# Decay masks by biased exponentials on ScalarE instead of subtractions and products on VectorE

## The chip, the cores and the metric

The kernel runs on one core of a Trainium2 chip. The metric is the device time of one execution in microseconds (us). The engines are named as in the profile: PE (TensorE matmul) and PEld (its weight loads), DVE (VectorE), ACT (ScalarE), POOL (GpSimd) and SP (SyncE, which issues the DMAs). Each engine runs its instructions in the order in which the program gives them, and an instruction that waits holds up all behind it on its engine.

## The reference

The model is two layers of a backbone for 256 context and 512 latent tokens of width 1024. In each layer one input projection feeds four head groups in parallel: A, windowed attention with a sink logit per head; B, dense attention; C, a bidirectional mLSTM in chunks; D, a bidirectional Mamba-2 in chunks of 128 tokens. Their outputs go through one output projection, and a squared-ReLU MLP follows.

Three things matter here. In A the softmax of a head is taken with one more logit, the sink: with m = max(scores/8, sink), the row is exp(score/8 - m), and its sum has exp(sink - m) added. In D, for each head h and direction d, the contribution of token s to token t of a chunk is weighted by

```
mask[s, t] = exp(cum[t] - cum[s]) * dt[s]      for t >= s (forward) or t <= s (backward), else 0
```

where cum is a running sum of decays and dt = softplus(...) is the step size. In C the weight is exp(-(b[s, t] - a[s])) with the same triangles. Since dt > 0, the D mask can also be written as exp(cum[t] + (ln dt[s] - cum[s])).

## The kernel before

Tokens are held in six chunks of 128 (two of context, four of latents). Layer 0 makes output for all six, layer 1 (`need` is False) for the four latent chunks. The head groups run one after the other, A first, then D, C and B; dense projections of a later group are cut into pieces and put between the steps of the group that runs (`fill(...)`), so that PE has work while DVE and ACT prepare the next step. Then come output projection and MLP, which are almost all matmuls. The program is written in the order of the dependences; a scheduler with priorities sets the final order of each engine's instructions, and pools of tiles (CB, MB and pr share one of four buffers) set when a buffer is free again.

The names that the change and the prediction touch:

- `attend_s` (from L619): scores and softmax of a pair of heads. `m` is the row maximum, `es` the sink's term, `pr` the probabilities, `den` (dn in the trace) their sum, `R` its reciprocal. `attend_v` transposes the probabilities into `pth`, `ptl` and multiplies by V; then `tm` and `yA` are A's output.
- `gates()` (L798 to L888): a generator whose steps are run between others. It makes `u` (48 columns of gate logits and 48 of dt), `cum`, `aS`, `D3`, later `E` and `crP`; rows of cumulative sums go to a DRAM buffer, `drv`.
- `fD` and `thd`: D's projections after convolution and gate. `btok`, `xtok`: their transposes. `hst`: the state of D. `adr`: a piece of the modulation.
- The D loop (L1026 to L1070), per chunk j: `CB` (128 x 2 directions x 4 heads x 128) is loaded by DMA as broadcast rows of cum, POOL fills the wrong triangle with -1e30 (L1033, L1034), DVE subtracts cum per partition, ACT takes the exponential, DVE (layer 0) or POOL (layer 1) multiplies by dt and adds the directions to `W`; DVE multiplies W by the raw product, and PE multiplies W by `xtok`. `yi` and `ysk` lead to `zs`; after the loop `zs` is scaled by `ssD` (L1073), transposed and evacuated to `yD`.
- The C loop (L1255 on), per chunk: `MB` is loaded and filled likewise, DVE subtracts `aS`, ACT takes the exponential, DVE multiplies by the raw product. `yC` is C's output; `qB`, `kB` and `bsq` belong to the projections of B that run beside it.

The helpers L95 (`mm`), L103 (`act`), L106 (`tt`), L110 and L111 (`ts`) and L114 (`stt`) record most instructions, so lines of the trace are often those.

Of the kernel before, what the change touches and what calls it, by code (L numbers as in the profile page):

```python
# [9 lines left out]
I32 = mybir.dt.int32  # L10
# [12 lines left out]
DEPTH = 2  # L23
EPS = 1e-6
BIG = 1e30

C_BADA, C_G1, C_G2, C_CW, C_CB, C_GM, C_GS, C_GB, C_GF = 0, 48, 56, 64, 82, 88, 90, 92, 94
NPC = 102
# [15 lines left out]
def tile_hybrid_backbone(ctx, tc, xin, cin, wada, wopen, win0, win, wout, wf1, wf2, pcol, prow, cst, rope, out):  # L44
# [444 lines left out]
    for l in range(DEPTH):  # L489
# [123 lines left out]
            return rp  # L613

        eos, khl = {}, {}
        gb = pc_[:, C_GB:C_GB + 2]
        rq = sm((P, NJ, 4), "rq")

        def attend_s(a, kv, j):  # L619
# [17 lines left out]
            for e in range(2):  # L637
                sp = s2()
                q = eo[:, e, js]
                for b in range(nb):  # L640
                    segs = []
                    lo_, hi_ = b * half, (b + 1) * half
                    if lo_ < NX:
                        segs.append((0, lo_, min(hi_, NX) - lo_))
                    if hi_ > NX:
                        s0 = max(lo_, NX)
                        segs.append((s0 - lo_, b0 + s0 - NX, hi_ - s0))
                    if len(segs) == 2 and segs[1][1] == segs[0][1] + segs[0][2]:
                        segs = [(0, segs[0][1], segs[0][2] + segs[1][2])]
                    mms = []  # L650
                    for part in range(2):
                        for o_, s_, n_ in segs:
                            mms.append((sp[:, b, o_:o_ + n_], q, KH[:, part, s_:s_ + n_]))
                    if a == "A":
                        for i, bl in enumerate(blocks):
                            if bl >= 2 and bl != j:
                                mk = mkp if bl < j else mkn
                                k0, k1 = i * P, (i + 1) * P
                                s0, s1 = max(k0, lo_), min(k1, hi_)
                                if s0 < s1:  # L660
                                    mms.append((sp[:, b, s0 - lo_:s1 - lo_], idb, mk[:, s0 - k0:s1 - k0]))
                    for i, (o_, l_, r_) in enumerate(mms):
                        mm(o_, l_, r_, i == 0, i == len(mms) - 1)
                sv = sp[:, 0:nb, 0:half]
                me, de = m1[:, e:e + 1], den[:, e:e + 1]
                hd = 2 * kv + e
                V.tensor_reduce(me, sv, AX.XY, ALU.max)
                if a == "A":
                    sk = pr_[:, R_SINK + hd:R_SINK + hd + 1]
                    ts(me, me, 0.125, sk, ALU.mult, ALU.max)  # L670
                    tt(es[:, e:e + 1], sk, me, ALU.subtract)
                    ts(me, me, -1.0, None, ALU.mult)
                    scale = 0.125
                else:
                    scale = rq[:, j, hd:hd + 1]
                    stt(me, me, -1.0, scale, ALU.mult, ALU.mult)
                pr = k4((P, nk), name="pr")
                act(pr.rearrange("p (b n) -> p b n", b=nb), sv, AF.Exp, bias=me, scale=scale, accum=de)
                Ps.append(pr)
            if a == "A":  # L680
                act(es, es, AF.Exp)
                tt(den, den, es, ALU.add)
            V.reciprocal(den, den)
            R = th_((P, P), name="R")
# [113 lines left out]
        def gates():  # L798
# [18 lines left out]
            act(an, pr_[:, R_ALOG:R_ALOG + 8], AF.Exp)  # L817
            ts(X[:, :, 0:8], u[:, :, 0:8], -1.0, None, ALU.mult)
            stt(X[:, :, 8:16], u[:, :, 8:16], -1.0, an.unsqueeze(1).to_broadcast([P, NJ, 8]), ALU.mult, ALU.mult)
            yield  # L820
            cp = bulk((P, 192))
            mm(cp[:, 0:48], cs[:, K_LE:K_LE + P], X[:, :, 0::2])
# [62 lines left out]
            V.tensor_copy(D3[:, 2], tot[:, :, 8:16])  # L885
            act(D3, D3, AF.Exp)
            tt(D3[:, 1], D3[:, 1], dt[:, :, 8:16], ALU.mult)
            yield  # L888

        gsteps = gates()  # L890
# [136 lines left out]
        for ji, j in enumerate(out_tok):  # L1027
# [4 lines left out]
                         drv[2:4, j * 512:(j + 1) * 512].unsqueeze(0).to_broadcast([P, 2, 512]))  # L1032
            G.affine_select(out=CB[:, 0], in_=CB[:, 0], pattern=[[0, 4], [1, P]], compare_op=ALU.is_ge, fill=-BIG, base=0, channel_multiplier=-1)  # L1033
            G.affine_select(out=CB[:, 1], in_=CB[:, 1], pattern=[[0, 4], [-1, P]], compare_op=ALU.is_ge, fill=-BIG, base=0, channel_multiplier=1)  # L1034
            tt(CB, CB, bc(cum[:, j, 8:16].rearrange("p (h d) -> p d h", d=2), (P, 2, 4, P)), ALU.subtract)
            act(CB, CB, AF.Exp)
            W_ = ta((P, 4, P), name="W")
            GV = V if need else G
            GV.tensor_tensor(CB, CB, bc(dt[:, j, 8:16].rearrange("p (h d) -> p d h", d=2), (P, 2, 4, P)), ALU.mult)
            GV.tensor_tensor(W_, CB[:, 0], CB[:, 1], ALU.add)  # L1040
            Wg = W_.rearrange("p (g h) t -> p g h t", g=2)
            tt(Wg, Wg, raw.unsqueeze(2).to_broadcast([P, 2, 2, P]), ALU.mult)
            fill(wa * fD_)
# [23 lines left out]
        yD = k6(4, (P, 2, NT), name="yD")  # L1067
        for j in out_tok:
            js = slice(j * P, (j + 1) * P)
            ts(zs[:, j, :], zs[:, j, :], ssD[:, j:j + 1], None, ALU.mult)  # L1070
            yp = mx((P, 256))
            for m in range(2):
                TE.transpose(yp[:, m * P:(m + 1) * P], zs[:, j, m * P:(m + 1) * P], ident)  # L1073
# [181 lines left out]
        for ji, j in enumerate(out_tok):  # L1255
# [4 lines left out]
            SY.dma_start(MBf, drv[0:2, j * 512:(j + 1) * 512].unsqueeze(0).to_broadcast([P, 2, 512]))  # L1260
            G.affine_select(out=MB[:, 0], in_=MB[:, 0], pattern=[[0, 4], [1, P]], compare_op=ALU.is_ge, fill=BIG, base=0, channel_multiplier=-1)
            G.affine_select(out=MB[:, 1], in_=MB[:, 1], pattern=[[0, 4], [-1, P]], compare_op=ALU.is_ge, fill=BIG, base=0, channel_multiplier=1)
            tt(MB, MB, bc(aS[:, j].rearrange("p (h d) -> p d h", d=2), (P, 2, 4, P)), ALU.subtract)
            act(MB, MB, AF.Exp, scale=-1.0)
            MBe = MB.rearrange("p d (e q) t -> p d e (q t)", e=2)
            tt(MBe, MBe, raw[:, :, 0:256].unsqueeze(1).to_broadcast([P, 2, 2, 256]), ALU.mult)
            fill(wa * fC_ if ji < nout - 1 else FILL_CB[l][4])
# [330 lines left out]
```

## Time and profile before

| | before |
|---|---|
| runs, median (lowest, highest) | 1860.95 us (1854.97, 1861.11) |
| profiled execution, own time | 1865.19 us |
| its span | 1862.9 us |
| mean granted PE clock | 0.969 |
| PE, DVE, ACT, POOL busy | 1776.5, 1227.1, 866.1, 331.4 us |

Busy time is an average over the whole span. It doesn't tell how the stages differ: in the MLP PE is the only engine that counts, and among the head groups the engines wait for each other. The granted clock is a share of 2.4 GHz. A wait is put down to the instruction that released it last.

### The profile page before, as it was taken

How to read it: one execution, taken by the hardware profiler on the slowest of the kernel's cores; microseconds unless marked ns; L12 is line 12 of the kernel's file. 1: busy time of each engine (PE TensorE's matmuls, PEld its weight loads, DVE VectorE, ACT ScalarE, POOL GpSimd, SP SyncE). 2: the span in 40 equal slices, each digit the busy share in tenths (PEclk: the TensorE clock that was granted, in tenths of full speed). 3: DMA queues.
4: the chain of work that ended last, by engine and by line, in shares of the span. 5: the costliest groups of instructions: out<-in, count | busy, mean ns of one | idle time of the engine just before them, and what ended most of it. 6: DMA issues, size and time to landing. Idle time of an engine off the chain costs nothing.

```text
span 1862.9 us, 31119 instructions
## 1 busy us (share of the span) xinstructions
PE 1776.5 (95%) x11754; PEld 1556.4 (84%) x11754; DVE 1227.1 (66%) x2765; ACT 866.1 (46%) x1820; POOL 331.4 (18%) x322
## 2 busy tenths in 40 slices
PE   7999999989999999999999989989989899999997
PEld 4898888878788888888888888879768799999997
DVE  3588875688877566466466576886588765555555
ACT  4655523356656464344345356542456543333333
POOL 1200111220014363142243311033120200000000
PEclk8999999799999999999999989999989899999999
DMA  8233442321123343342332411132221122332222
GB/s 315 80 103 105 147 129 86 104 97 52 35 80 109 97 130 102 97 130 97 100 121 97 138 62 53 46 93 86 74 69 52 40 91 92 96 96 92 91 93 66
DMA packets 97813, 178.85 MB, mean 96 GB/s; under 512 B 10752, under 2 KB 19328, under 8 KB 97664
## 3 DMA queue, kind: packets, MB, share of 16 engines
q1 hardware_dynamic: 97664, 176.88, 29.8%
q8 instruction: 92, 1.51, 0.3%
q14 instruction: 57, 0.47, 0.1%
HBM read 172.51 MB, written 4.33 MB: 95 GB/s over the span
## 4 chain that ended last, share of the span: by engine, by line
PE 79%; DVE 8%; ACT 5%; DMA 3%; issue 2%; POOL 2%; SPq 0%; DVEq 0%; ACTq 0%; POOLq 0%
PE bulk L95 39%; PE s L95 29%; PE mx L95 8%; PE mx L706 2%; ACT wh L103 1%; DVE wl L106 1%; DMA CB<-drows 1%; DVE x L114 1%; DMA adar<-in_wada_dram 1%; ACT qs L103 1%; POOL acc L296 1%; ACT pr L103 1%; DMA x<-in_xin_dram 1%; ACT pth L103 0%; DVE EO L106 0%
## 5 line engine op out<-in xcount | busy, mean ns | idle before, releaser
L106 DVE TENSOR_TENSOR wl<-wraw,wh 128x512 fp32r<-128x512 f32 (+2 forms) x400 | 286.5, 721 | 117.1 <-ACT wh L103 109.2
L103 ACT ACTIVATE wh<-wraw 128x512 fp32r<-128x512 f32 (+2 forms) x400 | 239.6, 610 | 265.4 <-PE bulk L95 139.4
L95 PE MATMUL s<-h,wh 128*128 128x258 f32 (+2 forms) x1040 | 316.6, 314 | 0.0
L95 PE MATMUL s<-hl,wh 128*128 128x258 f32 (+2 forms) x1040 | 305.9, 313 | 0.0
L95 PE MATMUL s<-h,wl 128*128 128x258 f32 (+2 forms) x1040 | 252.1, 312 | 0.0
L95 PE MATMUL bulk<-ah,wh 128*128 128x512 f32 (+1 forms) x576 | 218.1, 379 | 4.1 <-DVE mod L106 2.8
L95 PE MATMUL bulk<-ah,wl 128*128 128x512 f32 (+1 forms) x576 | 215.9, 375 | 0.0
L95 PE MATMUL bulk<-al,wh 128*128 128x512 f32 (+1 forms) x576 | 215.8, 375 | 0.0
L296 POOL TENSOR_TENSOR acc<-acc,adap 128x512 f32<-128x512 f32 x96 | 142.3, 1489 | 410.6 <-ACT acc L103 238.9
L95 PEld LDWEIGHTS s<-h,wh 128*128 128x128 f32 x1040 | 197.2, 190 | 20.8
L114 DVE SCALAR_TENSOR_TENSOR x<-bulk,mod,x 128x512 f32<-128x512 f32 (+1 forms) x224 | 149.4, 670 | 98.4 <-PE bulk L95 97.3
L95 PEld LDWEIGHTS s<-hl,wh 128*128 128x128 f32 x1040 | 197.7, 190 | 11.8 <-issue 0.2
L95 PEld LDWEIGHTS s<-h,wl 128*128 128x128 f32 x1040 | 165.9, 190 | 1.3
L95 PE MATMUL bulk<-h,wh 128*128 128x512 f32 (+1 forms) x416 | 154.2, 371 | 0.9 <-DVE KHL L106 0.5
L95 PE MATMUL bulk<-hl,wh 128*128 128x512 f32 (+1 forms) x416 | 145.3, 349 | 0.0
L95 PE MATMUL bulk<-h,wl 128*128 128x512 f32 (+1 forms) x416 | 145.2, 349 | 0.0
L95 PEld LDWEIGHTS bulk<-ah,wh 128*128 128x128 f32 x576 | 108.3, 188 | 25.3 <-DVE mod L106 4.6
L95 PEld LDWEIGHTS bulk<-ah,wl 128*128 128x128 f32 x576 | 108.2, 188 | 21.3
L95 PEld LDWEIGHTS bulk<-al,wh 128*128 128x128 f32 x576 | 108.3, 188 | 19.3
L103 ACT ACTIVATE relu<-relu,bs 128x512 f32<-128x512 f32 x96 | 58.8, 644 | 127.6 <-DVE relu L106 127.6
L103 ACT ACTIVATE adap<-adar,silw 128x256 f32<-128x256 f32 x192 | 85.0, 497 | 52.5 <-DMA adar<-in_wada_dram 52.5
L95 PE MATMUL bulk<-wh,h 128*128 128x256 f32 (+1 forms) x336 | 105.4, 314 | 3.0 <-ACT h L103 1.7
(355 smaller groups left out, 3809.1 us busy)
## 6 DMA issues: line engine op xcount, KB each, us to landing
wraw<-in_wf_dram SPq DMA_DIRECT2D x256, 256.0 KB, 2.7
adar<-in_wada_dram SPq DMA_DIRECT2D x96, 256.0 KB, 3.0
wraw<-in_win_dram SPq DMA_DIRECT2D x72, 256.0 KB, 2.9
ada<-in_wada_dram SPq DMA_DIRECT2D x64, 256.0 KB, 4.1
adaw<-in_wada_dram SPq DMA_DIRECT2D x16, 512.0 KB, 6.7
wraw<-in_wout_dram SPq DMA_DIRECT2D x32, 256.0 KB, 3.1
x<-in_xin_dram SPq DMA_DIRECT2D x8, 768.0 KB, 5.4
CB<-drows SPq DMA_DIRECT2D x10, 512.0 KB, 6.0
```

Of the source, the lines that this page charges most:

```text
L95: return TE.matmul(o, lhsT=l, rhs=r, start=start, stop=stop)
L103: return S.activation(o, i, f, scale=scale, **kw)
L106: return V.tensor_tensor(o, a, b, op)
L114: return V.scalar_tensor_tensor(o, a, s, b, op0, op1)
L296: G.tensor_tensor(acc[:, v], acc[:, v], dst, ALU.add)
L706: TE.transpose(tp[:, i, e, :], Ps[e][:, (i0 + i) * P:(i0 + i + 1) * P], ident)
```

## The change

The step size goes into the exponent. `gates()` computes ln(dt) by two Newton steps from a guess out of dt's bits, and keeps u = ln(dt) - cum in the columns of `u` that are free by then. In the D loop the subtraction of cum and the product by dt are gone; one exponential of 1024 columns is replaced by eight of 128, one for each direction and head, with u (a value per partition) as bias. In the C loop the subtraction of aS is gone in the same way. The sum of the two directions, W, is made by DVE in both layers. The scale of zs by ssD goes from DVE to ACT. In A's softmax the negated sinks are prepared once (`nsk`), and three small DVE operations per head become one; the sink's exponential is taken per head, with a bias.

```diff
--- before.py
+++ after.py
@@ -23,6 +23,7 @@
 DEPTH = 2
 EPS = 1e-6
 BIG = 1e30
+LN2 = 0.6931471805599453
 
 C_BADA, C_G1, C_G2, C_CW, C_CB, C_GM, C_GS, C_GB, C_GF = 0, 48, 56, 64, 82, 88, 90, 92, 94
 NPC = 102
@@ -613,6 +614,8 @@
             return rp
 
         eos, khl = {}, {}
+        nsk = sm((P, 4), "nsk")
+        ts(nsk, pr_[:, R_SINK:R_SINK + 4], -1.0, None, ALU.mult)
         gb = pc_[:, C_GB:C_GB + 2]
         rq = sm((P, NJ, 4), "rq")
 
@@ -666,10 +669,8 @@
                 hd = 2 * kv + e
                 V.tensor_reduce(me, sv, AX.XY, ALU.max)
                 if a == "A":
-                    sk = pr_[:, R_SINK + hd:R_SINK + hd + 1]
-                    ts(me, me, 0.125, sk, ALU.mult, ALU.max)
-                    tt(es[:, e:e + 1], sk, me, ALU.subtract)
-                    ts(me, me, -1.0, None, ALU.mult)
+                    ts(me, me, -0.125, nsk[:, hd:hd + 1], ALU.mult, ALU.min)
+                    act(es[:, e:e + 1], nsk[:, hd:hd + 1], AF.Exp, bias=me, scale=-1.0)
                     scale = 0.125
                 else:
                     scale = rq[:, j, hd:hd + 1]
@@ -678,7 +679,6 @@
                 act(pr.rearrange("p (b n) -> p b n", b=nb), sv, AF.Exp, bias=me, scale=scale, accum=de)
                 Ps.append(pr)
             if a == "A":
-                act(es, es, AF.Exp)
                 tt(den, den, es, ALU.add)
             V.reciprocal(den, den)
             R = th_((P, P), name="R")
@@ -817,6 +817,14 @@
             act(an, pr_[:, R_ALOG:R_ALOG + 8], AF.Exp)
             ts(X[:, :, 0:8], u[:, :, 0:8], -1.0, None, ALU.mult)
             stt(X[:, :, 8:16], u[:, :, 8:16], -1.0, an.unsqueeze(1).to_broadcast([P, NJ, 8]), ALU.mult, ALU.mult)
+
+            ln, d_ = u[:, :, 0:8], e[:, :, 0:8]
+            ts(d_, u[:, :, 8:16], 1e-30, None, ALU.max)
+            ts(ln, d_.bitcast(I32), LN2 / 8388608.0, -126.955 * LN2, ALU.mult, ALU.add)
+            for _ in range(2):
+                act(z[:, :, 0:8], ln, AF.Exp, scale=-1.0)
+                tt(z[:, :, 0:8], z[:, :, 0:8], d_, ALU.mult)
+                stt(ln, z[:, :, 0:8], -1.0, ln, ALU.add, ALU.add)
             yield
             cp = bulk((P, 192))
             mm(cp[:, 0:48], cs[:, K_LE:K_LE + P], X[:, :, 0::2])
@@ -885,6 +893,7 @@
             V.tensor_copy(D3[:, 2], tot[:, :, 8:16])
             act(D3, D3, AF.Exp)
             tt(D3[:, 1], D3[:, 1], dt[:, :, 8:16], ALU.mult)
+            tt(u[:, :, 0:8], u[:, :, 0:8], cum[:, :, 8:16], ALU.subtract)
             yield
 
         gsteps = gates()
@@ -1032,12 +1041,11 @@
                          drv[2:4, j * 512:(j + 1) * 512].unsqueeze(0).to_broadcast([P, 2, 512]))
             G.affine_select(out=CB[:, 0], in_=CB[:, 0], pattern=[[0, 4], [1, P]], compare_op=ALU.is_ge, fill=-BIG, base=0, channel_multiplier=-1)
             G.affine_select(out=CB[:, 1], in_=CB[:, 1], pattern=[[0, 4], [-1, P]], compare_op=ALU.is_ge, fill=-BIG, base=0, channel_multiplier=1)
-            tt(CB, CB, bc(cum[:, j, 8:16].rearrange("p (h d) -> p d h", d=2), (P, 2, 4, P)), ALU.subtract)
-            act(CB, CB, AF.Exp)
+            for d in range(2):
+                for h in range(4):
+                    act(CB[:, d, h, :], CB[:, d, h, :], AF.Exp, bias=u[:, j, 2 * h + d:2 * h + d + 1])
             W_ = ta((P, 4, P), name="W")
-            GV = V if need else G
-            GV.tensor_tensor(CB, CB, bc(dt[:, j, 8:16].rearrange("p (h d) -> p d h", d=2), (P, 2, 4, P)), ALU.mult)
-            GV.tensor_tensor(W_, CB[:, 0], CB[:, 1], ALU.add)
+            tt(W_, CB[:, 0], CB[:, 1], ALU.add)
             Wg = W_.rearrange("p (g h) t -> p g h t", g=2)
             tt(Wg, Wg, raw.unsqueeze(2).to_broadcast([P, 2, 2, P]), ALU.mult)
             fill(wa * fD_)
@@ -1067,7 +1075,7 @@
         yD = k6(4, (P, 2, NT), name="yD")
         for j in out_tok:
             js = slice(j * P, (j + 1) * P)
-            ts(zs[:, j, :], zs[:, j, :], ssD[:, j:j + 1], None, ALU.mult)
+            act(zs[:, j, :], zs[:, j, :], AF.Copy, scale=ssD[:, j:j + 1])
             yp = mx((P, 256))
             for m in range(2):
                 TE.transpose(yp[:, m * P:(m + 1) * P], zs[:, j, m * P:(m + 1) * P], ident)
@@ -1260,8 +1268,9 @@
             SY.dma_start(MBf, drv[0:2, j * 512:(j + 1) * 512].unsqueeze(0).to_broadcast([P, 2, 512]))
             G.affine_select(out=MB[:, 0], in_=MB[:, 0], pattern=[[0, 4], [1, P]], compare_op=ALU.is_ge, fill=BIG, base=0, channel_multiplier=-1)
             G.affine_select(out=MB[:, 1], in_=MB[:, 1], pattern=[[0, 4], [-1, P]], compare_op=ALU.is_ge, fill=BIG, base=0, channel_multiplier=1)
-            tt(MB, MB, bc(aS[:, j].rearrange("p (h d) -> p d h", d=2), (P, 2, 4, P)), ALU.subtract)
-            act(MB, MB, AF.Exp, scale=-1.0)
+            for d in range(2):
+                for h in range(4):
+                    act(MB[:, d, h, :], MB[:, d, h, :], AF.Exp, scale=-1.0, bias=aS[:, j, 2 * h + d:2 * h + d + 1])
             MBe = MB.rearrange("p d (e q) t -> p d e (q t)", e=2)
             tt(MBe, MBe, raw[:, :, 0:256].unsqueeze(1).to_broadcast([P, 2, 2, 256]), ALU.mult)
             fill(wa * fC_ if ji < nout - 1 else FILL_CB[l][4])
```

How the instructions move is shown at three places (the digits behind a name are the tile's number, x2 two instructions alike). First DVE's order in layer 1, where A's last output (yA) is made and the CB masks of the first chunks are due, before:

```order
L114 SCALAR_TENSOR_TENSOR fD_13706<-bulk_13653,cwh_12498,fD_13706 128x511
L114 SCALAR_TENSOR_TENSOR E_2320_12490<-E_2320_12490,cum_12492 128x48
L106 TENSOR_TENSOR CB_14207<-CB_14207,cum_12492 128x1024
L114 SCALAR_TENSOR_TENSOR fD_13706<-thd_13710,fD_13706 128x512
L110 TENSOR_SCALAR E_2320_12490<-E_2320_12490 128x48
L106 TENSOR_TENSOR tm_13749<-mx_13675,tm_13749 64x128 x2
L106 TENSOR_TENSOR wl_13795<-wraw_13796,wh_13794 128x512
L880 COPY crP_12496<-E_2320_12490 64x24
L881 COPY crP_12496<-E_2320_12490 64x24
L106 TENSOR_TENSOR yA_12500<-mx_13675,tm_13749 128x128
```

and after:

```order
L115 SCALAR_TENSOR_TENSOR fD_13733<-bulk_13680,cwh_12541,fD_13733 128x511
L111 TENSOR_SCALAR E_2322_12533<-E_2322_12533 128x48
L115 SCALAR_TENSOR_TENSOR fD_13733<-bulk_13680,cwh_12541,fD_13733 128x511
L888 COPY crP_12539<-E_2322_12533 64x24
L889 COPY crP_12539<-E_2322_12533 64x24
L107 TENSOR_TENSOR wl_13823<-wraw_13824,wh_13822 128x512
L115 SCALAR_TENSOR_TENSOR fD_13733<-thd_13737,fD_13733 128x512
L107 TENSOR_TENSOR tm_13777<-mx_13702,tm_13777 64x128 x2
L107 TENSOR_TENSOR wl_13829<-wraw_13830,wh_13828 128x512
L107 TENSOR_TENSOR yA_12543<-mx_13702,tm_13777 128x128
```

The subtraction of CB is gone from between fD's pieces; the copies to crP stand ahead of fD's product by thd, and one more wl stands ahead of yA.

The same stretch on ACT, before:

```order
L103 ACTIVATE fD_13706<-bulk_13653,cwh_12498 128x512
L103 ACTIVATE CB_14145<-CB_14145 128x1024
L103 ACTIVATE wh_13794<-wraw_13796 128x512
L103 ACTIVATE thd_13710<-fD_13706 128x512
L103 ACTIVATE tm_13749<-mx_13675 64x128 x2
L103 ACTIVATE wh_13800<-wraw_13802 128x512
L103 ACTIVATE CB_14207<-CB_14207 128x1024
L103 ACTIVATE E_2320_12490<-E_2320_12490 128x192
L103 ACTIVATE wh_13806<-wraw_13808 128x512
L103 ACTIVATE wh_13812<-wraw_13814 128x512
L103 ACTIVATE fD_13706<-bulk_13730,cwh_12498 128x512
```

and after:

```order
L104 ACTIVATE fD_13733<-bulk_13680,cwh_12541 128x512
L104 ACTIVATE CB_14173<-CB_14173,u_12538 128x128 x4
L104 ACTIVATE E_2322_12533<-E_2322_12533 128x192
L104 ACTIVATE wh_13822<-wraw_13824 128x512
L104 ACTIVATE thd_13737<-fD_13733 128x512
L104 ACTIVATE CB_14173<-CB_14173,u_12538 128x128
L104 ACTIVATE tm_13777<-mx_13702 64x128 x2
L104 ACTIVATE wh_13828<-wraw_13830 128x512
L104 ACTIVATE CB_14173<-CB_14173,u_12538 128x128 x3
L104 ACTIVATE wh_13834<-wraw_13836 128x512
L104 ACTIVATE CB_14240<-CB_14240,u_12538 128x128 x3
L104 ACTIVATE wh_13840<-wraw_13842 128x512
```

Four exponentials of the first CB tile stand ahead of the exponential of E; the others are spread between wh, thd and tm.

ACT where the first CB tile of layer 0 is made, before:

```order
L103 ACTIVATE wh_2782<-wraw_2784 128x512
L103 ACTIVATE tm_2689<-mx_2609 64x128 x2
L103 ACTIVATE thd_2666<-fD_2491 128x256
L103 ACTIVATE wh_2788<-wraw_2790 128x512
L103 ACTIVATE pth_2708<-mx_2702 128x512
L103 ACTIVATE wh_2794<-wraw_2796 128x512
L103 ACTIVATE wh_2800<-wraw_2802 128x512
L103 ACTIVATE fD_2491<-bulk_2677,cwh_974 128x512
L103 ACTIVATE tm_2758<-mx_2701 64x128 x2
L103 ACTIVATE CB_3252<-CB_3252 128x1024
```

and after:

```order
L104 ACTIVATE wh_2763<-wraw_2765 128x512
L104 ACTIVATE CB_3227<-CB_3227,u_973 128x128
L104 ACTIVATE pth_2683<-mx_2677 128x512
L104 ACTIVATE CB_3227<-CB_3227,u_973 128x128 x2
L104 ACTIVATE wh_2769<-wraw_2771 128x512
L104 ACTIVATE CB_3227<-CB_3227,u_973 128x128 x3
L104 ACTIVATE fD_2468<-bulk_2652,cwh_976 128x512
L104 ACTIVATE wh_2775<-wraw_2777 128x512
L104 ACTIVATE CB_3227<-CB_3227,u_973 128x128 x2
L104 ACTIVATE adrow_2726<-bulk_2709 128x128
L104 ACTIVATE tm_2733<-mx_2676 64x128 x2
```

One exponential of CB stands ahead of pth and five more between wh and the evacuation of fD, where before CB came behind fD and tm.

## Rows read from the trace of the kernel before

**Rows 1.** Page: busy us per engine, share of the span, instructions
```profile
...
PE 1776.5 (95%) x11754; PEld 1556.4 (84%) x11754; DVE 1227.1 (66%) x2765; ACT 866.1 (46%) x1820; POOL 331.4 (18%) x322
...
```

**Rows 2.** Windows: length, busy us (instructions) per engine, PE clock, DMA share, GB/s
```profile
...
440.00:1080.00 640.00, 632.75 (x3761) 551.31 (x3760) 406.97 (x738) 318.58 (x688) 193.70 (x160) 1.00 0.31 100
1220.00:1240.00 20.00, 16.07 (x85) 13.17 (x84) 16.40 (x30) 11.69 (x23) 9.71 (x10) 1.00 0.50 148
...
```

**Rows 3.** PE waits, layer 1, 1140 to 1420 us: total, times, longest
```profile
...
PE mx L991 <- DVE yA L106: 5.4, 1, 5.4
...
PE mx L1073 <- DVE zs L110: 1.5, 1, 1.5
...
```

**Rows 4.** PE waits, layer 0, 200 to 420 us
```profile
...
PE s L95 <- DVE W L106: 2.1, 2, 1.9
PE mx L1251 <- ACT yC L103: 1.7, 1, 1.7
PE bulk L95 <- DVE adr L217: 1.6, 2, 1.2
PE mx L95 <- DVE hst L106: 1.5, 1, 1.5
PE bulk L95 <- DVE qB L114: 1.1, 1, 1.1
...
PE mx L1073 <- DVE zs L110: 0.8, 1, 0.8
...
```

**Rows 5.** Timeline from 1229 us: start, us, what, [idle before <-releaser]
```profile
...
1232.02 0.74 DVE L114 SCALAR_TENSOR_TENSOR fD<-bulk,cwh,fD 128x511 f32<-128x511 f32 x1
...
1232.80 1.65 DVE L106 TENSOR_TENSOR CB<-CB,cum 128x1024 f32<-128x1024 f32 x1
...
1234.37 2.39 DVE L114 SCALAR_TENSOR_TENSOR fD<-thd,fD 128x512 f32<-128x512 f32 x1
...
1238.90 1.87 DVE L880 COPY crP<-E 64x24 f32<-64x24 f32 x1
...
1241.42 0.66 PE L991 MATMUL mx<-cst,fD 128*128 128x128 f32 x2 [5.35 <-DVE yA L106]
...
```

**Rows 6.** Tile CB: count, ns min/median/max, first and last start; waits
```profile
...
L106 DVE TENSOR_TENSOR CB<-CB,cum x10: 1212/1222/1654, 210.8 to 1251.8; 128x1024 f32<-128x1024 f32 x10
L103 ACT ACTIVATE CB<-CB x10: 1045/1060/1065, 212.9 to 1253.1; 128x1024 f32<-128x1024 f32 x10
L1039 DVE TENSOR_TENSOR CB<-CB,u x6: 1210/1216/1226, 218.0 to 277.1; 128x1024 f32<-128x1024 f32 x6
...
L1039 POOL TENSOR_TENSOR CB<-CB,u x4: 2065/2207/2872, 1233.3 to 1254.8; 128x1024 f32<-128x1024 f32 x4
...
  POOL CB L1033: 65.3, 7
...
```

**Rows 7.** Tile MB
```profile
...
L106 DVE TENSOR_TENSOR MB<-MB,aS x10: 1210/1218/2284, 281.9 to 1347.4; 128x1024 f32<-128x1024 f32 x10
...
```

**Rows 8.** Tile es
```profile
...
L106 DVE TENSOR_TENSOR es<-prow,m x40: 147/150/160, 96.7 to 1219.7; 128x1 f32<-128x1 f32 x40
...
```

**Rows 9.** Timeline from 298 us
```profile
...
298.32 1.67 DVE L110 TENSOR_SCALAR zs<-zs,ssD 128x256 f32<-128x256 f32 x6
...
299.20 3.51 ACT L103 ACTIVATE yD<-mx,pcol 128x128 f32<-128x128 f32 x12 [0.95 <-PE mx L1073]
...
```

**Rows 10.** Tile yD
```profile
...
L103 ACT ACTIVATE yD<-mx,pcol x20: 352/367/377, 299.2 to 1308.7; 128x128 f32<-128x128 f32 x20
...
```

**Rows 11.** Windows at the low granted clock
```profile
...
1240.00:1247.00 7.00, 5.58 (x26) 5.61 (x27) 5.83 (x12) 1.29 (x3) 0.73 (x1) 0.51 0.50 152
277.60:281.00 3.40, 3.40 (x18) 3.40 (x18) 3.40 (x6) 0.65 (x3) 1.21 (x2) 0.51 0.40 99
...
```

**Rows 12.** Timeline from 207.5 us, layer 0
```profile
...
208.73 0.58 ACT L103 ACTIVATE pth<-mx 128x512 fp32r<-128x512 f32 x1
...
210.13 0.63 POOL L1034 TENSOR_SCALAR_AFFINE_SELECT CB<-CB 128x512 f32<-128x512 f32 x1
...
```

## The prediction

> **What bounds the kernel now.** I read the page first, then a table of windows, then PE's waits in each layer, then the timeline around the longest ones. PE is busy 1776.5 us, 95% of the span [rows 1]. Between 440 and 1080 us it is busy 632.75 of 640 us at a granted clock of 1.00 [rows 2]: projections and FFN, where DVE and ACT have room. Nothing that the change takes from DVE there can move the end. What can be won lies where PE stands still for DVE, or runs at half clock after such a stop: the stretches of the head groups, 200 to 420 us and 1220 to 1400 us. The window 1220 to 1240 is the worst shown: PE 16.07 of 20 us, DVE 16.40, ACT 11.69 and POOL 9.71 [rows 2].
>
> In layer 1 the list of waits has one large entry: PE waits 5.4 us, once, for DVE's yA, and 1.5 us for DVE's zs [rows 3]. In layer 0 there are several small ones: W 2.1, adr 1.6, hst 1.5, qB 1.1 and zs 0.8, all behind DVE, and one behind ACT, yC, 1.7 [rows 4]. The timeline tells why the 5.35 us arise: DVE goes through its queue in order, and ahead of yA stand a CB subtraction of 1.65 us, an fD product of 2.39 us and a copy of 1.87 us. An fD operation of nearly the same shape takes 0.74 us just before [rows 5], and a small operation 0.15 us [rows 8].
>
> **The change, engine by engine.** DVE loses ten CB subtractions of 1.222 us (12.2 us) and six CB products of 1.216 us (7.3 us) [rows 6], ten MB subtractions of 1.218 us (12.2 us) [rows 7], 80 small softmax operations at 0.150 us (12.0 us) [rows 8] and ten zs scalings at 1.67/6 = 0.28 us (2.8 us) [rows 9]. It gains the four W additions of layer 1, half as long as a CB product, 0.6 us each by that row (2.4 us), and 14 small operations for ln(dt), 2.1 us at the softmax price. Net: 46.5 - 4.5 = 42 us off 1227.
>
> ACT pays. One exponential of 1024 columns, 1.060 us [rows 6], becomes eight of 128 columns with a bias per partition. Before has no exponential of that form. The nearest row is yD, a 128-column ACT operation with a scale per partition: 3.51 us for twelve back to back, 0.29 us each [rows 9]; alone, 0.377 us at most [rows 10]. The bound from below is the old price itself (eight pieces of 1060/8 ns, no gain or loss), from above 8 x 0.377 = 3.02 us. I take the row at its own cadence: 8 x 0.29 = 2.34 us, so 1.28 us more for each of 20 chunks, 25.6 us (0 to 39). The es exponentials go from 20 to 40 (20 more at some 0.2 to 0.3 us, 5 us), zs scaling comes at about 0.4 us each (estimate: yD has half the columns; 4 us), ln(dt) brings four small ones. In all some 35 us on 866: ACT is still under half busy, so the cost arises only where PE waits behind ACT.
>
> POOL loses four CB products of 2.207 us and the four W additions [rows 6]. Its affine selections and the loads that feed them stay, and SP issues as many DMAs as before. The selections' consumer changes: now an ACT exponential stands behind them, no longer a DVE subtraction. POOL waited 65.3 us in seven places for CB's load [rows 6]; where a load is late, ACT now waits with its whole queue behind it.
>
> **Where PE gets time back.** The 5.35 us in layer 1. PE goes on at 1241.42, so it had stood since 1236.07 [rows 5], and yA has to come that much earlier. Off DVE's queue go one CB subtraction wholly within the chain (1.65 us) and the one ahead of it (1.22 us by the median), together 2.87 us. fD and the copy ran while POOL multiplied CB by dt; with POOL's products gone they fall back to 0.74 and some 0.2 us, another 1.65 + 1.67 = 3.3 us. Against it: four exponentials of CB now stand ahead of the exponential of E in ACT's order, 4 x 0.29 = 1.2 us, and the copies and yA come behind E. So 2.87 + 3.3 - 1.2 = 5.0 us (1.7 if the slowing was not POOL's; 5.35 if E isn't late).
>
> The Trainium skill, "SBUF — State Buffer", section "SBUF: two separate sides", says that a VectorE operation reading two SBUF inputs and GpSimd exclude each other, and the loser stands wholly still. The fD product, two SBUF inputs, agrees with it: 2.39 us against 0.74. By subtraction of the removed operations alone the gain would be 1.7 us; by that rule it is 5.0.
>
> The clock behind it. From 1240 to 1247 the granted clock is 0.51, the 1.2 GHz level, after PE had stood for 5.35 us; 277.6 to 281 shows the same after the W wait [rows 11]. At half speed they cost about half their length, 3.4 and 1.7 us. If PE doesn't stop, I expect most of that back: 2.5 (0 to 3.4) and 1.1 (0 to 1.7). Other half-clock stretches I leave as they are.
>
> Layer 0: the hst wait of 1.5 us and the W wait, 1.9 at its longest, each stand behind one of the slowed CB subtractions, which take up to 1.654 us [rows 6]. They go from DVE; the exponentials end 1.28 us later on ACT by their own length, but start 1.6 us earlier. 1.2 (0 to 1.5) and 1.9 (0.5 to 2.1). The two zs waits (0.8 and 1.5): DVE drops MB subtractions ahead of the chain that ends in the scale, and the scale itself goes to ACT, where an MB exponential can stand in front. Of 2.3 us I take half, 1.2 (-0.5 to 2.3). The qB wait of 1.1 us stands behind an MB subtraction, the one that took up to 2.284 us [rows 7]: 0.7 (-0.5 to 1.1).
>
> Losses. At the start of layer 0's CB work ACT now has one CB exponential ahead of pth. Pth began at 208.73 us, while the second selection of that CB ended only at 210.13 + 0.63 = 210.76 [rows 12]: if that exponential waits for it, pth, and the P x V product behind it, come some 2 us later. PE has filler work there, and the adr wait of 1.6 us shrinks, since its CB subtraction goes: -0.6 (-2 to +0.5). Where PE waits for ACT already (yC, and its like in layer 1), a wait can grow by 1.28 us: -1.0, of -2.6 for two. The softmax head of group A I count at nothing: per pair of heads DVE saves four small operations and ACT adds one, but PE has dense projections to fill with there; without that cover it would be a few tenths per head either way. The ln(dt) operations cost nothing: in the changed order the last of them stands 140 DVE rows ahead of the first W of layer 1; without that slack, a chain of eight at 0.15 to 0.2 us, 1.5 us per layer.
>
> Sum: 5.0 + 2.5 + 1.2 + 1.9 + 1.1 + 1.2 + 0.7 - 0.6 - 1.0 = 12.0 us. With all terms at their ends, from a loss of 4 to a gain of 17.5. The profiled execution took 1865.19 us, 4.2 above the median of 1860.95 of the runs; off it the sum gives 1853.2, at the level of the runs 1848.95. I predict 1849.
>
> A price from the notes by itself: the Trainium skill, "ScalarE: Activation LUTs", section "What ACT_TABLE_LOAD costs", puts an activation with a pointer bias at 280 ns + 0.833 ns per column, some 93 ns of it hidden back to back. That would make eight exponentials 2.4 us (estimate), against 2.34 by yD's cadence; no exponential with a bias of this size is in this trace.
>
> **Rivals.** First, the gain is hidden: the exponentials come late on ACT just where the subtraction was late on DVE, since both wait for the same load and selection. For it: CB's consumers lose 1.28 us of what the subtraction (1.22) gave; against it: the large stall is of things queued behind the subtraction, not of CB itself. Then 5.0 shrinks to 1.7, the clock stays, W and hst give nothing, tails nothing: about 0 to 3 us, 1858 to 1861.
>
> Second, slower: ACT's queue becomes the bound. The place is each CB or MB chunk whose load is late (seven waits of CB at POOL, some 9 us each on average): ACT stands at the first exponential and behind it the evacuations (pth, fD, btok) on which PE's PSUM buffers hang. With 1.28 us of new work and a wait of up to 2 us at pth's place, ten of 20 chunks that reach PE would cost 10 x 2 = 20 us; less the 8 us that the yA place and its clock still give, 12 us: 1872. It decides from about six such places on. Against it: ACT is busy 11.69 of 20 us in the worst window shown, and the scheduler's order puts pieces of the exponentials between the evacuations.
>
> Third, more than I count: with PE no longer stopping, other half-speed stretches go too, or DVE's 42 us thin out waits that the lists show below 1 us. Some 10 us more: 1839. For it, the two stretches in [rows 11]; against it, others come with PE busy throughout.
>
> **How the numbers follow.** Forecast (1843 to 1856) 0.55, hidden 0.22, slower 0.11, more 0.12. A difference under 0.5%, 9.3 us, can't be told from none: faster means under 1851.6. Three quarters of the forecast's case and the last rival lie there: 0.41 + 0.12 = 0.53. Slower: 0.11 and a remainder, 0.12. Same: 0.35. The range 1838 to 1866 leaves out part of the last rival and most of the slower one; by the forecast's own bounds alone it would be 1843.5 to 1865.
>
> **What would show it.** Right: no PE wait for yA above 1 us in layer 1, fD and the copies at 0.7 and 0.2 us there, full clock just behind, W and hst gone from the waits of layer 0. An eight-piece exponential at 2.2 to 2.5 us. Wrong: PE waits for pth, fD, kB or bsq on ACT of over 1 us in several chunks, ACT waiting for POOL's selections with PSUM evacuations queued behind, or half-clock stretches that only moved.

## The result, and the profile after

The changed kernel takes 1846.73 us (median of 20 runs, 1840.83 to 1855.68), the one before 1859.25 us (20 runs, 1854.97 to 1861.57). The ratio is 0.9939, with a 95% interval of 0.9928 to 0.9951: 11.3 us less (9.1 to 13.4), 12.5 by the medians. The forecast was 12.0 us less, 1849 us, in a range of 1838 to 1866.

The page after, busy us of each engine as in [rows 1]:

```profile
...
PE 1767.9 (96%) x11754; PEld 1549.0 (84%) x11754; DVE 1181.5 (64%) x2669; ACT 899.3 (49%) x1994; POOL 317.2 (17%) x314
...
```

DVE has lost 45.6 us (42 in the sum) and ACT gained 33.2 (35). PE still bounds the kernel. The mean granted clock is 0.977 in this profile, 0.969 in the one before.

The list of PE's waits in layer 1, 1140 to 1420 us (total, times, longest), answers to [rows 3]:

```profile
...
PE s L96 <- DVE W L107: 3.3, 2, 2.9
...
PE mx L1000 <- DVE xtok L1004: 1.3, 2, 0.8
...
```

The same for layer 0, 200 to 420 us, answers to [rows 4]:

```profile
...
PE bulk L96 <- DVE adr L218: 3.0, 2, 2.0
...
PE mx L1259 <- ACT yC L104: 1.7, 1, 1.7
...
PE bulk L96 <- DVE qB L115: 0.5, 1, 0.5
...
```

The wait for yA is gone, and so are those for hst and W in layer 0 and for zs on DVE. New or longer are W in layer 1 (3.3 us, one of 2.9) and adr in layer 0 (3.0, before 1.6); smaller ones are x in layer 0 (1.6, before 0.3), qB behind ACT there (0.9, new) and fD in layer 1 (1.1, new).

The stretch around yA in the timeline answers to [rows 5]:

```profile
...
1219.67 1.28 ACT L104 ACTIVATE CB<-CB,u 128x128 f32<-128x128 f32 x4 [1.33 <-POOL CB L1042]
...
1221.23 0.17 DVE L888 COPY crP<-E 64x24 f32<-64x24 f32 x1 [0.91 <-ACT E L104]
...
1221.88 1.06 POOL L1042 TENSOR_SCALAR_AFFINE_SELECT CB<-CB 128x512 f32<-128x512 f32 x1 [1.66 <-DMA CB<-drows]
...
1222.37 1.12 DVE L115 SCALAR_TENSOR_TENSOR fD<-thd,fD 128x512 f32<-128x512 f32 x1
...
1224.75 0.29 DVE L107 TENSOR_TENSOR yA<-mx,tm 128x128 f32<-128x128 f32 x1
...
1225.18 0.41 PE L1000 MATMUL mx<-cst,fD 128*128 128x128 f32 x2
...
1226.73 0.44 PE L1000 MATMUL mx<-cst,fD 128*128 128x128 f32 x2 [0.78 <-DVE xtok L1004]
...
1230.72 0.68 DVE L115 SCALAR_TENSOR_TENSOR fD<-thd,fD 128x512 f32<-128x512 f32 x1
...
```

The copies to crP take 0.17 us each, fD 1.12 us instead of 2.39, and PE doesn't stop at its next transposition (1225.18). Two waits for xtok of 0.78 and 0.56 us are what is left.

The operations that changed, by tile. CB, answering to [rows 6]:

```profile
...
L104 ACT ACTIVATE CB<-CB,u x80: 385/393/407, 205.8 to 1235.8; 128x128 f32<-128x128 f32 x80
...
L107 DVE TENSOR_TENSOR W<-CB x10: 684/984/1180, 245.4 to 1278.1; 128x512 f32<-128x512 f32 x10
...
  POOL CB L1042: 65.6, 7
  ACT CB L104: 8.6, 4
...
```

zs, which was [rows 9], and es, which was [rows 8]:

```profile
...
L104 ACT ACTIVATE zs<-zs,ssD x10: 493/498/523, 287.2 to 1291.8; 128x256 f32<-128x256 f32 x10
...
```

```profile
...
L104 ACT ACTIVATE es<-nsk,m x40: 277/287/299, 92.3 to 1207.2; 128x1 f32<-128x1 f32 x40
...
```

Eight pieces of 0.393 us stand for each 1.060 us of before, back to back four in 1.28 us (at 1219.67 in the timeline above). POOL waits for CB's load as long as before (65.6 us), and ACT now waits for POOL behind it, 8.6 us in four places (at MB, 21.8 us in nine). W's addition takes DVE 0.98 us by the median, not 0.6; the six that DVE made in layer 0 before had taken 1.11 by the median.

The windows of the granted clock, in the first microseconds and behind the places of the two large waits, answer to [rows 11]:

```profile
...
14.80:28.50 13.70, 8.91 (x111) 5.38 (x112) 6.76 (x26) 7.61 (x16) 0.45 (x1) 0.98 1.04 403
1228.00:1235.00 7.00, 6.44 (x55) 6.24 (x55) 5.18 (x13) 6.92 (x25) 0.00 (x0) 1.00 0.20 64
1280.70:1284.00 3.30, 3.30 (x12) 2.91 (x12) 2.85 (x6) 1.09 (x4) 0.00 (x0) 0.50 0.83 180
...
```

Behind yA's place PE keeps the full clock; it has the low one, 1.2 GHz, just behind the new W wait. The first of these windows belongs to no change: the profile of before had the low clock there,

```profile
...
14.80:28.50 13.70, 11.26 (x90) 6.68 (x90) 3.06 (x17) 3.96 (x9) 0.00 (x0) 0.50 1.03 402
...
```

and the 200th matmul of PE came at 38.5 us, against 34.6 after. So 4 of the 17.0 us between the two spans are the start of this one execution. The rest, 13, is near the 11.3 of the runs.

Since both kernels run 11754 matmuls in nearly the same order, the starts of the same-numbered ones show where time goes (negative: gained):

| matmuls, place | after less before, us |
|---|---|
| 200 to 1800, A and gates of layer 0 | -0.4 |
| 1800 to 2000, hst | -1.7 |
| 2000 to 2200, W and the clock behind it | -4.0 |
| 2200 to 2400, end of D, adr, zs | +1.7 |
| 2400 to 3200, C of layer 0 | -1.9 |
| 3200 to 7800, MLP, start of layer 1 | -0.5 |
| 7800 to 8000, yA and the clock behind it | -6.0 |
| 8000 to 8400, end of D in layer 1 | +3.8 |
| 8400 to 9000, C of layer 1 | -1.5 |
| 9000 to 9200, start of B in layer 1 | -1.8 |

Single profiles differ in this table by more than the edits, in C of layer 0 above all. Two kernels of the next section are edited in layer 1 alone (no CB subtraction, no POOL product there), and both come through the matmuls 2400 to 3200 faster than the profile of before, by 3.9 and 2.9 us; from 310 to 420 us the granted clock is 0.89 in both, 0.86 in before. So the -1.9 us of C in layer 0 can't be put down to the change.

### The profile page after: what moved, and what is told of

Same layout as the page of the kernel before. It is cut to its first block, busy times and chain, and to the rows that moved or that the text cites. A ratio compares the mean times of both kernels' runs of the same rounds, so it can differ in the third digit from the quotient of the medians.

```text
span 1845.9 us, 31190 instructions
## 1 busy us (share of the span) xinstructions
PE 1767.9 (96%) x11754; PEld 1549.0 (84%) x11754; DVE 1181.5 (64%) x2669; ACT 899.3 (49%) x1994; POOL 317.2 (17%) x314
## 4 chain that ended last, share of the span: by engine, by line
PE 77%; DVE 8%; ACT 5%; POOL 3%; DMA 3%; issue 3%; SPq 0%; DVEq 0%; ACTq 0%; POOLq 0%
PE bulk L96 37%; PE s L96 29%; PE mx L96 7%; PE mx L706 2%; POOL acc L297 1%; DMA adar<-in_wada_dram 1%; ACT wh L104 1%; DVE wl L107 1%; ACT qs L104 1%; DVE x L115 1%; DMA CB<-drows 1%; DMA MB<-drows 1%; DMA x<-in_xin_dram 1%; ACT adap L104 0%; DVE EO L107 0%
## 5 line engine op out<-in xcount | busy, mean ns | idle before, releaser
L107 DVE TENSOR_TENSOR wl<-wraw,wh 128x512 fp32r<-128x512 f32 (+2 forms) x400 | 282.5, 711 | 119.8 <-ACT wh L104 110.2
```

Of the source, the lines that this page charges most:

```text
L107: return V.tensor_tensor(o, a, b, op)
```

## The experiments

All are timed against the kernel before on the same chip; differences in us are the ratio's, with its 95% interval.

| kernel | ratio (interval) | us |
|---|---|---|
| D masks alone | 0.9965 (0.9951 to 0.9978) | -6.5 |
| C masks alone | 0.9965 (0.9951 to 0.9980) | -6.5 |
| softmax head alone | 0.9982 (0.9969 to 0.9995) | -3.3 |
| zs on ACT alone | 1.0013 (1.0000 to 1.0025) | +2.4 |
| before, no CB subtraction in layer 1 | 0.9990 (0.9980 to 0.9999) | -1.9 |
| before, no POOL product in layer 1 | 0.9969 (0.9955 to 0.9982) | -5.8 |
| before, all mask exponentials in eight | 0.9957 (0.9945 to 0.9970) | -8.0 |
| before, C's exponentials in eight | 0.9982 (0.9970 to 0.9995) | -3.3 |
| before, no subtraction in C | 0.9954 (0.9939 to 0.9969) | -8.6 |
| after, W of layer 1 on POOL | 0.9900 (0.9883 to 0.9918) | -18.6 |
| after, ysk and yi of layer 1 on DVE | 0.9914 (0.9898 to 0.9930) | -16.0 |
| after, W on POOL and zs on DVE | 0.9892 (0.9875 to 0.9909) | -20.1 |

**The parts alone.** Each part of the diff was put into the kernel before without the others.

```diff
D masks alone:  gates(): ln(dt), u - cum;  D loop: exponentials with bias u, W on DVE
C masks alone:  - tt(MB, MB, aS, subtract);  act(MB, exp)
                + eight act(MB[:, d, h, :], exp, bias=aS)
head alone:     nsk, one ts per head, es by act with bias
zs alone:       - ts(zs, zs, ssD, mult)   + act(zs, zs, Copy, scale=ssD)
```

> Only D's masks are changed (ln(dt) in the exponent, eight exponentials with bias, W added on DVE). Theory: the gain lies where CB's subtraction and product stood in front of other work, so this part alone gives most of it: -8 to -11 us of the -12.5, the 5.4 us wait for yA goes, hst and W waits of layer 0 go, and the new W wait of layer 1 (2.9 us) appears. Rival (the gain follows the DVE time taken away, 17 of 42 us here): about -5 us.

> Only C's masks are changed (no subtraction of aS, eight exponentials with bias). Theory: DVE's subtraction holds up PE only in the qB wait of 1.1 us and near the zs waits: -1 to -3 us; the yA wait of 5.4 us stays. Rival by DVE time (12 of 42 us): -3.6 us.

> Only the softmax head of A is changed. Theory: PE has dense projections to fill with there, 0 +- 1.5 us. Rival by DVE time (12 of 42 us): -3.6 us. The yA wait of 5.4 us stays in both.

> Only the scale of zs goes from DVE to ACT. Theory: 0 +- 1 us: the two zs waits (0.8 and 1.5 us) end with the rsqrt chain before the scale, whichever engine scales. Rival by DVE time (3 of 42 us): -0.8 us. Second rival (ACT is the slower one for this and its queue is in front): +1 to +2 us.

Measured: -6.5, -6.5, -3.3 and +2.4, together -13.9, within the error of the whole change's -11.3. My theory for the shares was wrong for C and the head, and the rival by DVE time was nearer there, though too small for C; for D the result lies between the two (-5 and -8) and decides nothing, and for zs the second rival, that ACT is the slower one, came nearest. In the D part's profile the wait for yA is 0.4 us and the new W wait 2.4, as expected: what was gained at yA (6.7 us by the numbered matmuls) was half given back at W (3.6). In the head's profile gains and losses of up to 3 us in D and C cancel: apart from the start, its last matmul comes within 0.1 us of before's. Its -3.3 is not located in any place.

zs on ACT is slower by itself, by an interval (0.0 to 4.6 us) that reaches down to nothing. ACT takes 0.498 us for a scale that took DVE 0.348 in the profile of before, and PE's waits in layer 1 in the zs kernel say where it lands:

```profile
...
PE mx L1073 <- ACT yD L103: 1.6, 1, 1.6
PE mx L1073 <- ACT zs L103: 1.3, 1, 1.3
...
```

Before it waited there once for DVE, 1.5 us; now for ACT twice, 2.9 us.

**What held yA up.** Two kernels each leave out one of the two suspects in layer 1.

```diff
-            tt(CB, CB, bc(cum...), ALU.subtract)
+            if need:
+                tt(CB, CB, bc(cum...), ALU.subtract)
```

> The kernel before with the four CB subtractions of layer 1 left out (the D mask of that layer then lacks its -cum[s]); POOL still multiplies by dt. Theory (the yA wait is made of two parts, DVE's own subtractions, 2.87 us, and the slowing of fD and of the copy while POOL multiplies, 3.3 us): the wait for yA falls from 5.4 to about 2.5 us, and fD or its neighbours stay slow (over 1.5 us) beside POOL's products; time -2 to -4 us. Rival (DVE's subtractions alone make the wait): under 0.5 us.

```diff
-            GV.tensor_tensor(CB, CB, bc(dt...), ALU.mult)
+            if need:
+                GV.tensor_tensor(CB, CB, bc(dt...), ALU.mult)
```

> The kernel before with POOL's four products by dt of layer 1 left out (the D mask of that layer then lacks its dt[s]); DVE still subtracts. Theory: fD back to 0.7 us and the copy to 0.2 us, the yA wait falls from 5.4 to about 2 us; time -2 to -5 us. Rival (DVE's own work alone makes the wait; POOL doesn't touch DVE): the wait stays above 4.5 us, fD stays at 2.4 us.

Without the subtractions, the timeline shows the second crP copy beside POOL's product:

```profile
...
1229.78 1.90 POOL L1040 TENSOR_TENSOR CB<-CB,u 128x1024 f32<-128x1024 f32 x1
...
1229.85 1.87 DVE L881 COPY crP<-E 64x24 f32<-64x24 f32 x1
...
1233.43 0.29 DVE L106 TENSOR_TENSOR yA<-mx,tm 128x128 f32<-128x128 f32 x1
...
1233.64 3.10 DVE L106 TENSOR_TENSOR wl<-wraw,wh 128x512 fp32r<-128x512 f32 x2
...
1233.87 4.64 POOL L1040 TENSOR_TENSOR CB<-CB,u 128x1024 f32<-128x1024 f32 x2
1233.87 0.66 PE L991 MATMUL mx<-cst,fD 128*128 128x128 f32 x2 [2.52 <-ACT wh L103]
...
1237.14 0.69 PE L991 MATMUL mx<-cst,fD 128*128 128x128 f32 x2 [1.97 <-DVE xtok L995]
...
```

POOL's product runs from 1229.78 to 1231.68, and a copy of 64 x 24 elements on DVE from 1229.85 to 1231.72: it ends when POOL does. There is no wait for yA in this kernel's list, but the place is the same: PE stands from 1231.35, yA is ready at 1233.72 and wh only at 1233.87, so the 2.5 us are put down to wh, which came last. By yA alone they would be 2.4, as the theory had it. Just behind, DVE takes 3.10 us for two wl operations beside POOL's next products, so that xtok is late and PE stands another 2.0 us. The time falls by 1.9 us only. Without POOL's products, and with the subtractions in place, the same stretch reads:

```profile
...
1228.69 1.11 DVE L114 SCALAR_TENSOR_TENSOR fD<-thd,fD 128x512 f32<-128x512 f32 x1
...
1231.48 0.16 DVE L880 COPY crP<-E 64x24 f32<-64x24 f32 x1
...
1231.66 0.17 DVE L881 COPY crP<-E 64x24 f32<-64x24 f32 x1
...
1232.30 0.41 PE L991 MATMUL mx<-cst,fD 128*128 128x128 f32 x2 [2.06 <-DVE yA L106]
...
```

The copies are back to 0.16 us, fD to 1.11, and the wait for yA is 2.06 us of 5.35, as the theory had it; the time falls by 5.8 us. So POOL's product holding up DVE was worth 3.3 us of that wait and DVE's own subtractions 3.0, each taken away alone; in time POOL's is the larger share, since its products also hold up what follows.

**ACT's price.** The exponentials in eight pieces without any relief for DVE:

```diff
-            act(CB, CB, AF.Exp)
+            for d in range(2):
+                for h in range(4):
+                    act(CB[:, d, h, :], CB[:, d, h, :], AF.Exp)
```

and the same for MB.

> The kernel before, with each exponential of CB and MB in eight pieces of 128 columns and no bias; the subtractions and products stay. ACT's price by itself, about 1.2 us for each of 20 chunks. Theory: ACT has room, 0 to +3 us. Rival (ACT's queue in front of the evacuations costs PE time): +6 us or more.

It was expected to cost a little; it gains 8.0 us. ACT's extra work costs less than the pieces give, which let other work through: the scheduler puts wh and thd between them. In its timeline

```profile
...
1226.93 0.62 ACT L103 ACTIVATE wh<-wraw 128x512 fp32r<-128x512 f32 x1
...
1231.32 1.11 DVE L114 SCALAR_TENSOR_TENSOR fD<-thd,fD 128x512 f32<-128x512 f32 x1
...
1232.36 0.16 DVE L880 COPY crP<-E 64x24 f32<-64x24 f32 x1
...
1232.62 1.90 POOL L1041 TENSOR_TENSOR CB<-CB,u 128x1024 f32<-128x1024 f32 x1 [0.73 <-ACT CB L103]
...
1235.53 0.66 PE L991 MATMUL mx<-cst,fD 128*128 128x128 f32 x2 [3.76 <-DVE yA L106]
...
```

a wh stands after the first piece, POOL's product starts only behind the copies to crP, and the wait for yA is 3.76 us. By the numbered matmuls it gains 2.6 us there, 1.5 in C of layer 1 and 2.2 at the start of B, and loses 2.4 at W in layer 0. The 4.1 us in C of layer 0 are no more than the kernels edited in layer 1 alone show there, so the rest of the 8.0 isn't located.

**C: pieces or subtraction.** After that run I suspected that in C the pieces alone did it. One kernel has only MB's exponentials in eight (the subtraction stays), the other only lacks the subtraction.

```diff
C in eight:        - act(MB, MB, AF.Exp, scale=-1.0)   + eight act(MB[:, d, h, :], ..., scale=-1.0)
no subtraction:    - tt(MB, MB, bc(aS...), ALU.subtract)
```

> The kernel before with only C's exponentials in eight pieces (no bias); the subtraction of aS stays on DVE. Theory, new (in C it is the pieces that help, by where the scheduler puts the work around them, and not the subtraction that goes): -4 to -7 us, as with the whole change of C's masks (-6.5), with the same gains in C of layer 1 and in B behind it. Rival (DVE's subtraction was what held C up): 0 +- 1.5 us.

> The kernel before with C's subtraction left out (the mask of C then lacks aS[s]) and the one exponential of 1024 columns kept. New theory (the pieces help): 0 to -2 us. Rival (the subtraction held C up): -5 to -7 us.

The suspicion fell: -3.3 and -8.6 us. The subtraction that goes is worth the more, and the pieces give something too, but the two don't add up (-6.5 with both, -11.9 as a sum). One place of the difference is the end of D in layer 1, where the subtraction stood inside the chain that makes ssD. DVE's timeline of before:

```profile
...
1301.97 0.17 DVE L111 TENSOR_SCALAR rv<-ssD 128x4 f32<-128x4 f32 x1
...
1302.39 0.16 DVE L111 TENSOR_SCALAR ry<-rv 128x4 int32<-128x4 int32 x1
1302.46 1.22 DVE L106 TENSOR_TENSOR MB<-MB,aS 128x1024 f32<-128x1024 f32 x1
1303.59 0.15 DVE L106 TENSOR_TENSOR rw<-ry 128x4 f32<-128x4 f32 x1
...
1305.36 0.88 DVE L110 TENSOR_SCALAR zs<-zs,ssD 128x256 f32<-128x256 f32 x3
```

Without it the chain from rv to zs (1291.90 to 1294.30) has none of MB between its links:

```profile
...
1291.90 0.17 DVE L111 TENSOR_SCALAR rv<-ssD 128x4 f32<-128x4 f32 x1
...
1292.32 0.16 DVE L111 TENSOR_SCALAR ry<-rv 128x4 int32<-128x4 int32 x1
1292.52 0.17 DVE L106 TENSOR_TENSOR rw<-ry 128x4 f32<-128x4 f32 x1
...
1294.30 1.14 DVE L110 TENSOR_SCALAR zs<-zs,ssD 128x256 f32<-128x256 f32 x4
...
```

2.4 us instead of 3.4, and PE's list has no wait for zs. The numbered matmuls tell the two apart: at the end of D in layer 1 both kernels without the subtraction gain 1.9 us and the pieces alone lose 1.8; in C of layer 1 both kernels with pieces gain 1.4 to 1.5 and the one without them nothing. At the start of B all three (C masks, pieces, no subtraction) gain 1.8 to 2.2 us, though no mask work stands there, which fits another layout by the scheduler but isn't shown. How much of C's gain is this isn't settled.

**The new wait for W.** In the changed kernel, W of layer 1's last chunk is late. The timeline there:

```profile
...
1261.52 1.18 DVE L107 TENSOR_TENSOR W<-CB 128x512 f32<-128x512 f32 x1
...
1275.93 0.63 POOL L1269 TENSOR_SCALAR_AFFINE_SELECT MB<-MB 128x512 f32<-128x512 f32 x1 [5.13 <-DMA MB<-drows]
...
1277.12 0.61 POOL L1066 TENSOR_TENSOR ysk<-xtok,prow 128x256 f32<-128x256 f32 x1
...
1277.77 0.42 DVE L107 TENSOR_TENSOR ysk<-ysk,s 128x256 f32<-128x256 f32 x1 [2.58 <-POOL ysk L1066]
1278.10 0.86 DVE L107 TENSOR_TENSOR W<-CB 128x512 f32<-128x512 f32 x1
...
1280.37 1.74 PE L96 MATMUL s<-xtok,W 128*128 128x64 f32 x8 [2.92 <-DVE W L107]
...
```

POOL waits 5.13 us for MB's load; ysk's product stands behind MB's selections, DVE waits 2.58 us for it, and W stands behind ysk on DVE. Before, POOL made W, the second one at

```profile
...
1269.22 1.31 POOL L1040 TENSOR_TENSOR W<-CB 128x512 f32<-128x512 f32 x1 [1.06 <-PE mx L95]
...
```

This is 13.0 us ahead of the matmuls that use it (1282.18); DVE now makes it 3.8 us ahead of them (1261.52, 1265.32). CB and MB share buffers, and MB's load is issued as this W is finished (before at 1270.56, after at 1262.77): a later W makes MB's load, POOL's selections, ysk and the next W later in turn. The last W of before stood behind MB's selections as well (1290.83) and was in time. Two kernels undo it in different ways.

```diff
W on POOL:         - tt(W_, CB[:, 0], CB[:, 1], ALU.add)
                   + (V if need else G).tensor_tensor(W_, CB[:, 0], CB[:, 1], ALU.add)
ysk, yi on DVE:    - G.tensor_tensor(ysk, xtok, D, mult)   + (G if need else V).tensor_tensor(...)
                   - G.tensor_tensor(yif0, yif0, yif1, add)   + (G if need else V).tensor_tensor(...)
```

> The changed kernel with W's addition in layer 1 back on POOL, as before. Theory (the new 2.9 us wait for W in layer 1 arises since DVE's W stands behind ysk, which waits for a POOL operation behind the selections of MB): the wait for W falls below 1 us and the time is about 3 us less than the changed kernel's (-15 us against before). Rival (POOL's addition, 1.3 to 2.3 us, comes no earlier, as it stands behind the same selections): the same time as the changed kernel, -12.

> The changed kernel with the product ysk and the addition to yi of layer 1 on DVE instead of POOL, W's addition staying on DVE. Theory (W on DVE stands behind ysk, and ysk behind POOL's selections of MB): the wait for W in layer 1 falls from 2.9 us below 1, the time by about 3 us to -15 against before. Rival (W on DVE is late by itself, since DVE is the slower place for it): the wait stays above 2 us, the time at -12.

Both remove the wait: W is gone from the list for layer 1 with W on POOL, and down to 0.2 us with ysk on DVE. There W stays on DVE and isn't late, so it was the place behind POOL's queue and not DVE's speed. They gain 7.3 and 4.7 us over the changed kernel's -11.3; by the intervals, some 4 us either way, neither is clear of the 3.8 us of W and its clock. In their profiles C of layer 0 is faster, too, by 3.3 and 3.5 us. The order of instructions in layer 0 is that of the changed kernel on every engine, and the granted clock from 310 to 420 us is 0.92 instead of 0.88: a difference of executions, as far as one profile each can tell.

**The best of it.** W on POOL, and zs back on DVE.

> The changed kernel with W's addition of layer 1 back on POOL and the scale of zs back on DVE: the two parts that cost time alone (+3.6 us at W in layer 1, +2.4 us for zs) undone. If they add up: -18.6 - 2.4 = -21 us against before. Rival (the adr wait of 2 us in layer 0 and the zs waits are of ACT's exponentials, not of the scale): -18, as with W alone.

1839.88 us (median of 4 runs), -20.1. It beats the kernel before and, by intervals that don't meet, the changed one; from W on POOL alone (-18.6) it can't be told apart. The wait for adr in layer 0 is 2.9 us in its list, as in the changed kernel's, so it isn't the scale's. The two kernels that only drop C's subtraction (C masks, no subtraction) have it, too, 2.9 and 3.0 us, and the D part alone has 1.5: the longer wait for adr comes with that subtraction's going.

## Why the prediction was right

The total came out (12.0 forecast, 11.3 or 12.5 measured), by terms of which several were off and cancel: W in layer 1 and the end of D were missed, C and the head gave more than the sum has. That the total fits so closely is luck; that its largest term came about as described is not.

- **yA and its clock: 5.0 + 2.5 forecast, 6.0 measured.** The five kernels that leave that place as it was differ there by 0.1 to 1.5 us from before. Right in its mechanism. The two runs that take one suspect away each show it: POOL's product is worth 5.4 - 2.1 = 3.3 us of the wait, as in the sum, and the subtractions 5.35 - 2.37 = 3.0 (2.87 in the sum). The page "SBUF — State Buffer" of the Trainium skill (section "SBUF: two separate sides") counts an fp32 copy from SBUF to SBUF, too, among the VectorE operations that lock GpSimd out and are locked out by it. The copy that ends with POOL's product agrees with it. fD came back to 1.12 us, not to the 0.74 that I expected: a POOL selection runs beside it (1221.88), and the same product takes 0.68 us where POOL is idle (1230.72). The granted clock behind yA's place is 1.00, where it was 0.51. 1.3 us of the term are lost to the xtok waits.
- **hst, W and its clock in layer 0: 1.2 + 1.9 + 1.1 = 4.2 forecast, 5.7 measured.** Right in kind; they went altogether. The 5.7 is rough, since the spot at W (2000 to 2200) moves by -1.5 us with the C masks alone and by +2.8 with the softmax head alone, which leave D as it is.
- **The zs waits: 1.2 forecast, in layer 0 a loss of 1.7 together with adr.** This step was half wrong. "DVE drops MB subtractions ahead of the chain" is right, as the kernel without them shows. But the scale on ACT gives nothing there (+2.4 us alone, 0.0 to 4.6). The loss of 1.7 is for the most part of this execution: the kernels with W on POOL and ysk on DVE, the same in layer 0, lose 0.4 and 0.2. The page "ScalarE: Activation LUTs" of the Trainium skill, section "Rules for kernel authors", gives such arithmetic to VectorE; 0.498 against 0.348 us agrees.
- **adr, -0.6 forecast.** The place I named was harmless: ACT stood 1.46 us at the exponential ahead of pth, and up to the 1800th matmul nothing is lost. The longer wait for adr (2.0 us at 287 us) came later, where adr stands on DVE behind the chain that makes ssD, and it comes with C's subtraction going.
- **W in layer 1: not in the sum at all.** I priced the move of the four additions from POOL to DVE by their length, 0.6 us each, where DVE's own in layer 0 had taken 1.11, and didn't ask what they then stand behind. It took 3.8 us with the clock: the largest miss.
- **C, 0.7 forecast.** Too small: -6.5 alone. I had counted only the one listed wait (qB), while the subtraction also stood in the chain to ssD in layer 1 (1.9 us by the numbered matmuls), and the C part's profile shows 1.5 us in C of layer 1 and 1.8 at the start of B besides.
- **The softmax head, 0 forecast, -3.3 (0.9 to 5.8) alone.** Not explained.
- **ACT's price.** Eight exponentials with bias are 0.393 us each alone and 1.28 us for four, so 2.4 to 2.6 us per chunk (2.34 in the sum). The rival in which ACT's queue becomes the bound fell: the kernel with the pieces and nothing else is faster.
- **Two sums.** The bounds of the terms add up to a loss of 3.4 us, given as 4, and the slower rival gives 1873 rather than 1872. Neither changes the forecast.

## What to carry to other kernels

A sum over listed waits finds where DVE's relief counts, but when an operation moves to another engine, ask what it will stand behind there: here the move of four additions of about 1 us each cost 3.8 us, and moving them back beat the change as a whole. An operation on POOL can hold up DVE's smallest copy for its full length, so look at what runs on POOL where DVE is on the path: the product beside yA was worth taking off, the addition to W was not. Cutting a long ACT instruction into pieces can pay by itself, since the scheduler can put urgent work between them; time it alone before crediting the rest of an edit.

## What the runs showed of the hardware

- A DVE copy of 64 x 24 elements took 1.87 us beside a POOL product of 1.90 us, and 0.16 us without it.
- POOL's selections and DVE hold each other up, too: DVE's fD product of 128 x 512 took 1.12 us beside a selection of 1.06 us, and 0.68 us with POOL idle; it took 1.11 us beside selections of 1.36 and 1.71 us in the kernels without POOL's products and with all exponentials in eight. Selections take 0.63 us at the least.
- In these runs the bias costs ACT about 0.1 us per instruction: 0.393 us for a 128 x 128 exponential with a bias per partition, 0.296 without, each alone. The Trainium skill, "ScalarE: Activation LUTs", section "What ACT_TABLE_LOAD costs", gives some 93 ns for a pointer operand; the 97 ns here agree. The tile view of the kernel with the pieces only:

```profile
...
L103 ACT ACTIVATE CB<-CB x80: 292/296/314, 210.9 to 1248.0; 128x128 f32<-128x128 f32 x80
...
```

- Runs of one kernel differ as their mean granted clock does: of 30 runs of the kernel before on one chip the fastest, 1850.6 us, had 0.981 and the slowest, 1865.33 us, 0.970. Part of the change's gain can be such clock: its 20 runs have a median of about 0.976, those 30 of before, from another set of runs, 0.973, and 0.003 of 1850 us is 5.6 us (an estimate, if all of it would have been work at the full clock).
